# Decoder trunk of one attention/state-space layer and one S5 layer: where the first layer's activations and the low weight parts lie in memory, modulo 256 bytes

## The chip, the cores and the metric

The kernel runs on one NeuronCore of a Trainium2 chip. The metric is the device time of one execution in microseconds (us). Three runs of the kernel before took 1301.74, 1299.94 and 1299.41 us; the median is 1299.94 us.

## The reference

Two post-norm layers on an activation matrix of 256 positions by 2048 channels, in float32. Each one ends in `x <- LayerNorm(alpha * x + mixer(x))`.

```python
# layer 0
z, xbc, dt, q, k, v, gate = jnp.split(x @ w_in, SPLITS0, axis=-1)   # 2048 x 13344
y_a = ...   # state-space scan over conv(xbc), dt; gated by silu(z); RMS norm
y_b = moba_attention(rope(q), rope(k), v) * jax.nn.silu(gate)
h = jnp.concatenate([y_a, y_b], axis=-1) @ w_out                    # 4096 x 2048
# layer 1
u, gate = jnp.split(x @ w_in, 2, axis=-1)                           # 2048 x 4096
y = jax.nn.gelu(s5_ssm(u, ...))
ga, gb = jnp.split(y @ w_glu, 2, axis=-1)                           # 2048 x 4096
h = (ga * jax.nn.sigmoid(gb) * jax.nn.silu(gate)) @ w_out           # 2048 x 2048
```

The matrix products with `w_in`, `w_out` and `w_glu` are nearly all of the arithmetic, and the change concerns how TensorE reads the operands of those with the two `w_in`.

## The kernel before

**Split products.** TensorE multiplies float32r numbers. To keep float32 accuracy, each operand is split into a high part (the value copied as float32r) and a low part (the value minus its high part). A product is then three terms: high by high, high by low, low by high. ScalarE writes the high parts of the weights (L244), VectorE the low parts (L252). A unit is 512 KB of weights, loaded by one DMA into a tile `raw` and split into two tiles `wh` and `wl`, each 128 partitions by 1024 elements (4096 bytes in a partition). The pool `st` holds four buffers each of `raw`, `wh` and `wl`; units are taken in order, three ahead.

**Two ways to multiply.** A matmul has a stationary operand of 128 x 128, which a weight load (PEld in the profile) brings into the array, and a moving operand, which streams past it.

- In `pairmm` (L336 to L344) the weights stand and the activations move. The activations' high and low parts lie in one tile (`x2`, index 0 and 1, each 16 k-tiles of 256 positions). For each weight block there are two matmuls. The one at L340 has a block of `wh` standing and streams 512 columns: 256 of the high part, then 256 of the low part, 16,384 bytes further on. The one at L343 has the block of `wl` standing and streams the 256 columns of the high part. These two are called a pair here, the long step and the short step. All of the first layer's input projection but `v` is made so, 176 units with 8 pairs each, and the `u` half of the second layer's, but for its first 512 columns: 24 units with 8 pairs each. In the first 208 units (`TURNS`) the scheduler alternates long and short steps wherever both weight parts are there; the first 8 units (bank names `aux`) still run in groups of up to four of a kind. From unit 208 on all long steps of a unit come first, then all short ones.
- In `xmm` (L327 to L334) the activations stand and the weights move, 512 columns at a time. `v` in the first layer (4 products of 8 units, each unit 12 matmuls: 384 in all) and the products with `w_out`, `w_glu` and the `gate` half are made so.

**Where things lie.** The buffer `AB` is allocated at L479 as `xx` for the first layer's input, and later again for `ya`, `y5` and `gb1`. `CF` holds the other activations, `x1t` (the second layer's input) among them. In the allocation of the program before, every tile of `AB`, `CF`, `wh` and `wl` begins at 64 bytes modulo 256. Within them, k-tiles lie 1024 bytes apart and weight blocks 512 bytes, so that modulo 256 all slices of one tile begin alike. One thing differs: the function `low_tile` (L210 to L213) makes `wl` 256 bytes longer and, for the units listed in `weights_stand` (L208: those in which the weights stand), takes a view of it that begins `SHIFT` = 16 elements, 64 bytes, into the tile. So where weights stand, `wh` begins at the same place as x modulo 256, and `wl` 64 bytes behind x.

**What sets the order.** The instruction order is made by a scheduler from the program's dependencies. With one exception at the very start, TensorE's instruction stream is never held back by the others for long; the profile below shows it.

Of the kernel before, what the change touches and what calls it, by code (L numbers as in the profile page):

```python
# [10 lines left out]
F32R = mybir.dt.float32r  # L11
# [5 lines left out]
P = 128  # L17
S = 256
D = 2048
KT = D // P  # L20
UK = 2
# [3 lines left out]
FAST = [2, 3]  # L25
STEPS = [0, 1, 4, 2, 5, 6, 3, 7]
WARM0 = 10
SHIFT = 16
TURNS = 208
FIRST = 3  # L30
EPS = 1e-5
# [140 lines left out]
def trunk(tc, io, out):  # L172
# [4 lines left out]
    def nm(s):  # L177
        count[0] += 1
        return f"{s}_{count[0]}"

    with ExitStack() as top:
# [3 lines left out]
        st = enter(tc.tile_pool(name="st", bufs=4))  # L185
# [19 lines left out]
        def big(tag, shape, dt=F32):  # L205
            return slot.tile(shape, dt, tag=tag, name=nm(tag))

        weights_stand = set(range(80)) | {80 + 32 * h + i for h in range(4) for i in range(32) if i // 8 != 2} | set(range(280, 304))  # L208

        def low_tile(n=None):  # L210
            at = SHIFT if n in weights_stand else 0
            t = st.tile([P, UK * 512 + 4 * SHIFT], F32R, tag="wl", name=nm("wl"))
            return t[:, at : at + UK * 512].rearrange("p (k n) -> p k n", n=512)  # L213

        units = []
        for name in ("wi0", "wo0", "wi1", "wglu", "wo1"):
            units += [io[name][i] for i in range(io[name].shape[0])]
# [18 lines left out]
        def chained(engine, f, *args, **kw):  # L236
            with inline(engine):
                ins = f(*args, **kw)
            line[engine] = ins
            return ins  # L240
# [8 lines left out]
        def split(n, raw, wh, wl, high=None):  # L249
            high = high or split_high(n, raw, wh)  # L250
            with inline(V):
                low = V.tensor_tensor(wl, raw, wh.bitcast(F32), op=OP.subtract)  # L252
            if V in line:
                line[V] = low
            splits[n] = (high, low)
            ready[n] = (wh, wl)
            nsplit[0] += 1

        def split_to(i):
            while nsplit[0] <= min(i, len(units) - 1):  # L260
                n = nsplit[0]
                if n in early:
                    early.pop(n)()
                if n in special:
                    special.pop(n)(n)
                    continue
                raw = st.tile([P, UK, 512], F32, tag="raw", name=nm("raw"))
                if n == 0:
                    wh = st.tile([P, UK, 512], F32R, tag="wh", name=nm("wh"))
                    wl = low_tile(n)  # L270
                    for k in range(UK):
                        chained(nc.sync, nc.sync.dma_start, raw[:, k, :], units[n][:, k * 512 : k * 512 + 512])
                    for k in range(UK):
                        xpart(k)
                        chained(A, A.activation, wh[:, k, :], raw[:, k, :], AF.Copy)
                        chained(V, V.tensor_tensor, wl[:, k, :], raw[:, k, :], wh[:, k, :].bitcast(F32), op=OP.subtract)
                    ready[n] = (wh, wl)
                    nsplit[0] += 1
                    continue
                if n == FIRST + 1:  # L280
                    for e in (nc.sync, A, V):
                        line.pop(e, None)
                f = chained if nc.sync in line else lambda e, f, *a: f(*a)
                lastraw[0] = f(nc.sync, nc.sync.dma_start, raw.rearrange("p k n -> p (k n)"), units[n])
                at = room.get(n, n)
                if at in keep[1]:
                    wh, wl = (keep[0].tile([P, UK, 512], F32R, tag=f"{t}{at % 8}", name=nm(t)) for t in ("wh", "wl"))
                else:
                    wh, wl = st.tile([P, UK, 512], F32R, tag="wh", name=nm("wh")), low_tile(n)
                split(n, raw, wh, wl)  # L290

        jobs = deque()
# [55 lines left out]
        def product_pairs(hl, wide=None):  # L348
            ps = wide or banks()
            nu = CU if wide else CU // 2  # L350
            for u in range(nu):
                split_to(unit[0] + 3)
                wpair = ready.pop(unit[0])
                if not wide:
                    wpair = [quads(t) for t in wpair]
                nj, last = 2 if wide else 4, u == nu - 1
                steps = [(j, o) for j in range(nj) for o in range(len(ps))]
                if last:
                    steps = [(j, o) for o in range(len(ps)) for j in range(nj)]
                with inline(T):  # L360
                    for part in ([steps[:nj], steps[nj:]] if last else [steps]):
                        for terms, (j, o) in ([(t, s) for s in part for t in ((0,), (1,))] if unit[0] < TURNS else [(t, s) for t in ((0,), (1,)) for s in part]):
                            pairmm(ps, wpair, j, o, hl(u * nj + j), u == 0 and j == 0, last and j == nj - 1, terms)
                unit[0] += 1
                pump(nu - 1 - u)
            return ps
# [24 lines left out]
        def product(kind, hl, nu=CU, prelude=None, late=None):  # L391
            ps = banks()
            for u in range(nu):
                if prelude:
                    prelude(u)
                split_to(unit[0] + 3)
                wpair = ready.pop(unit[0])
                if kind == "w":
                    wmm(ps, u, nu, hl, wpair, late if u == 0 else None)
                else:  # L400
                    last = u == nu - 1
                    steps = [(j, o) for o in range(2) for j in range(UK)] if last else [(j, o) for j in range(UK) for o in range(2)]
                    for j, o in steps:
                        xmm(ps, o, wpair, j, hl(u * UK + j), u == 0 and j == 0, last and j == UK - 1)
                unit[0] += 1
                pump(nu - 1 - u)
            return ps
# [68 lines left out]
            for i in range(n):  # L476
                T.matmul(px[:m, 0 : z.shape[1]], z[:, 0:m], z, start=i == 0, stop=i == n - 1)

        xx = big("AB", [P, 2, KT, S], F32R)  # L479
        xh, xl = xx[:, 0], xx[:, 1]  # L480
        wb = [dram.tile([P, 1792], F32, name=f"wb{b}") for b in range(16)]
        qd = dram.tile([4, P, P], F32, name="qd")
# [8 lines left out]
        with ExitStack() as l0:  # L491
# [31 lines left out]
            def xpart(k):  # L523
                xr = xr0[k]
                chained(A, A.activation, xh[:, k, :], xr, AF.Copy)
                chained(V, V.tensor_tensor, xl[:, k, :], xr, xh[:, k, :].bitcast(F32), op=OP.subtract)
# [773 lines left out]
        with ExitStack() as l1:  # L1300
# [287 lines left out]
            forms, fx, gp, set0 = more["f"], more["x"], more["p"], more["s"]  # L1588

            def fast_unit(raws, second):  # L1590
                def go(n):
                    raw = st.tile([P, UK, 512], F32, tag="raw", name=nm("raw"))
                    lastraw[0] = nc.sync.dma_start(raw.rearrange("p k n -> p (k n)"), units[n])
                    if not second:
                        wh, wl = st.tile([P, UK, 512], F32R, tag="wh", name=nm("wh")), low_tile()
                        raws[0] = raw
                        split(n, raw, wh, wl)
                        return
                    wh, wl = (fx.tile([P, 1, 512], F32R, tag=t, bufs=2, name=nm(t)) for t in ("bh", "bl"))
                    ra = raws[0]  # L1600
                    ta, tb = (fx.tile([P, 2, 512], F32, tag="mix", bufs=2, name=nm("mix")) for _ in range(2))
                    V.tensor_tensor(ta, ra, raw[:, 1:2, :].to_broadcast([P, 2, 512]), op=OP.subtract)
                    V.tensor_tensor(tb[:, 0, :], ta[:, 1, :], ra[:, 0, :], op=OP.add)
                    V.tensor_tensor(tb[:, 1, :], raw[:, 0, :], tb[:, 0, :], op=OP.subtract)
                    got = [(wh, wl)]
                    A.activation(wh[:, 0, :], raw[:, 0, :], AF.Copy)
                    V.tensor_tensor(wl[:, 0, :], raw[:, 0, :], wh[:, 0, :].bitcast(F32), op=OP.subtract)
                    for t, pool, bufs in ((ta, fx, 2), (tb, st, 4)):
                        th = pool.tile([P, UK, 512], F32R, tag="wh", bufs=bufs, name=nm("wh"))
                        tl = low_tile() if pool is st else fx.tile([P, UK, 512], F32R, tag="wl", bufs=2, name=nm("wl"))  # L1610
                        high = A.activation(th, t, AF.Copy)
                        low = V.tensor_tensor(tl, t, th.bitcast(F32), op=OP.subtract)
                        got.append((th, tl))
                    splits[n] = (high, low)
                    ready[n] = got
                    nsplit[0] += 1
                return go
# [260 lines left out]
```

## Time and profile before

| | |
|---|---|
| median of three runs | 1299.94 us |
| profiled execution, its own time | 1299.05 us |
| span of the profiled execution (first to last instruction) | 1297.3 us |
| TensorE busy | 1289.6 us (99%) |
| weight loads busy (they overlap the matmuls) | 1093.0 us (84%) |
| VectorE, ScalarE, GpSimd busy | 1042.0, 705.5, 422.7 us |
| granted TensorE clock, mean | 1.000 |

Matmuls are pipelined: a matmul is shown as busy until its last result has been written, so the durations of neighbours overlap. What a matmul costs in a stream is the time from its start to the start of the next one, and that is called a step here. The chain of waits gives the same as the duration of its pieces, and the timeline gives starts to 0.01 us, so that steps are best read over several in a row.

### The profile page before, as it was taken

What the parts mean: (1) busy time and instruction counts of PE and PEld (TensorE: products, weight loads), DVE (VectorE), ACT (ScalarE), POOL (GpSimd) and SP (SyncE); (2) the same over time, 40 slices, a digit from 0 to 9 for tenths busy, and PEclk for the clock granted to TensorE, in tenths of its full rate; (3) what the DMA queues carried; (4) which work ended last, traced back from release to release, by engine and by line L of the source; (5) the groups of instructions that cost most, each with busy time, mean ns of one, the idle gap of its engine ahead of it and who ended that gap; (6) DMA issues with size and microseconds to landing.
All of it is one profiled execution on the core that took longest, in us unless ns stands there. A gap on an engine that the chain in (4) does not pass through costs nothing.

```text
span 1297.3 us, 21557 instructions
## 1 busy us (share of the span) xinstructions
PE 1289.6 (99%) x7998; PEld 1093.0 (84%) x7998; DVE 1042.0 (80%) x1575; ACT 705.5 (54%) x974; POOL 422.7 (33%) x665
## 2 busy tenths in 40 slices
PE   9999999999999999999999999999999999999998
PEld 8888888887888888888888888888888888888886
DVE  6879948797799888889878766749998868878876
ACT  6657669974644544544654345643356545554442
POOL 0150000133029659748788720034433200000100
PEclk9999999999999999999999999999999999999999
DMA  8545675455557757858967777398988665556862
GB/s 326 185 161 179 207 272 195 156 186 180 205 189 248 260 184 263 270 177 256 328 212 259 234 270 255 131 324 271 322 307 296 212 214 191 181 182 225 284 228 89
DMA packets 92106, 295.47 MB, mean 228 GB/s; under 512 B 11536, under 2 KB 18704, under 8 KB 91744
## 3 DMA queue, kind: packets, MB, share of 16 engines
q1 hardware_dynamic: 73696, 249.57, 55.9%
q0 software_dynamic: 8224, 32.81, 7.7%
q10 hardware_dynamic: 10080, 11.71, 3.0%
q8 instruction: 63, 1.03, 0.3%
q14 instruction: 43, 0.35, 0.1%
HBM read 272.78 MB, written 21.27 MB: 227 GB/s over the span
## 4 chain that ended last, share of the span: by engine, by line
PE 95%; POOL 2%; DVE 1%; DMA 1%; ACT 0%; issue 0%; SPq 0%; POOLq 0%; ACTq 0%
PE main L332 37%; PE main L340 25%; PE main L343 13%; PE more L1632 7%; PE main L1632 3%; PE main L1270 2%; PE aux L963 1%; PE aux L340 1%; POOL CF L579 1%; PE aux L864 1%; POOL CF L580 1%; PE enc L1390 1%; PE dec L1435 1%; PE aux L468 1%; PE aux L1050 1%; PE aux L1083 1%
## 5 line engine op out<-in xcount | busy, mean ns | idle before, releaser
L252 DVE TENSOR_TENSOR wl<-raw,wh 128x1024 fp32r<-128x1024 f32 x425 | 530.6, 1254 | 194.0 <-ACT wh L244 189.0
L244 ACT ACTIVATE wh<-raw 128x1024 fp32r<-128x1024 f32 x425 | 446.8, 1057 | 435.0 <-PE main L332 177.4
L340 PE MATMUL main<-AB,wh 128*128 128x512 f32 x1344 | 470.8, 394 | 0.0
L343 PE MATMUL main<-AB,wl 128*128 128x256 f32 x1344 | 376.3, 280 | 0.0
L340 PEld LDWEIGHTS main<-AB,wh 128*128 128x128 f32 x1344 | 252.3, 188 | 54.8 <-issue 1.2
L343 PEld LDWEIGHTS main<-AB,wl 128*128 128x128 f32 x1344 | 255.1, 190 | 0.7 <-issue 0.4
L332 PE MATMUL main<-wh,CF 128*128 128x512 f32 (+1 forms) x768 | 240.0, 391 | 0.0
L332 PE MATMUL main<-wh,AB 128*128 128x512 f32 x640 | 201.8, 392 | 0.0
L332 PEld LDWEIGHTS main<-wh,CF 128*128 128x128 f32 x768 | 143.7, 188 | 30.0
L332 PE MATMUL main<-wl,CF 128*128 128x512 f32 x384 | 149.5, 389 | 0.0
L332 PEld LDWEIGHTS main<-wh,AB 128*128 128x128 f32 x640 | 120.0, 188 | 25.8 <-issue 0.6
L793 POOL TENSOR_TENSOR c<-c 128x8 f32<-128x8 f32 (+2 forms) x192 | 121.8, 652 | 38.5 <-DMA wb<-c 31.0
L332 PE MATMUL main<-wl,AB 128*128 128x512 f32 x320 | 124.7, 390 | 0.0
L332 PEld LDWEIGHTS main<-wl,CF 128*128 128x128 f32 x384 | 72.1, 188 | 14.6
L1632 PE MATMUL more<-wh,AB 128*128 128x512 f32 x228 | 76.8, 391 | 0.0
L795 POOL TENSOR_TENSOR c<-c,c 128x4 f32<-128x4 f32 (+2 forms) x96 | 68.1, 709 | 7.4
L332 PEld LDWEIGHTS main<-wl,AB 128*128 128x128 f32 x320 | 60.1, 188 | 12.1
L1030 POOL TENSOR_TENSOR a<-a,b 64x512 f32<-64x512 f32 x16 | 28.7, 1796 | 112.9 <-DVE a L1029 93.8
L972 POOL TENSOR_TENSOR ssq<-ssq,c 128x256 f32<-128x256 f32 x16 | 22.0, 1373 | 111.0 <-ACT c L970 110.3
L796 POOL TENSOR_TENSOR c<-c,c 128x4 f32<-128x4 f32 (+2 forms) x96 | 53.8, 561 | 0.0
L340 PE MATMUL main<-CF,wh 128*128 128x512 f32 x192 | 50.4, 396 | 0.0
L1632 PEld LDWEIGHTS more<-wh,AB 128*128 128x128 f32 x228 | 42.7, 188 | 8.8
(355 smaller groups left out, 1634.8 us busy)
## 6 DMA issues: line engine op xcount, KB each, us to landing
raw<-in_wi SPq DMA_DIRECT2D x271, 512.0 KB, 4.1
raw<-in_wo SPq DMA_DIRECT2D x96, 512.0 KB, 4.4
raw<-in_wglu SPq DMA_DIRECT2D x64, 512.0 KB, 3.3
wt<-wb POOLq DMA_DIRECT2D x16, 896.0 KB, 7.2
a<-cumd SPq DMA_DIRECT2D x8, 512.0 KB, 6.0
bc<-in_s5bc SPq DMA_DIRECT2D x16, 256.0 KB, 4.5
bt<-in_s5bt SPq DMA_DIRECT2D x16, 256.0 KB, 5.4
lt<-qd SPq DMA_DIRECT2D x32, 128.0 KB, 5.2
```

The source lines that it names most:

```text
L244: ins = A.activation(wh, raw, AF.Copy)
L252: low = V.tensor_tensor(wl, raw, wh.bitcast(F32), op=OP.subtract)
L332: end = T.matmul((ps[o] if acc is None else acc)[:, cs], l[:, k, sl], r[:, j, cs], start=start and i == 0, stop=stop and i == 2, skip_grou ...
L340: T.matmul(ps[o].rearrange("p (a n) -> p a n", a=2), wh[:, j, sl], x2[:, :, k, :], start=start, stop=False, skip_group_check=True)
L343: T.matmul(ps[o][:, 0:S], wl[:, j, sl], x2[:, 0, k, :], start=False, stop=stop, skip_group_check=True)
L793: G.tensor_tensor(p[:, :, :, 0:m], cs[:, :, :, 1 : m + 1], cs[:, i, :, n : n + 1].unsqueeze(1).to_broadcast([P, 2, 4, m]), op=OP.mult)
L795: G.tensor_tensor(cs[:, 0, :, n + 1 : n + 1 + m], p0[:, 0, :, 0:m], p1[:, 1, :, 0:m], op=OP.subtract)
L796: G.tensor_tensor(cs[:, 1, :, n + 1 : n + 1 + m], p0[:, 1, :, 0:m], p1[:, 0, :, 0:m], op=OP.add)
L972: G.tensor_tensor(ssq, ssq, jk[:, f, :], op=OP.add)
L1030: turns.append(G.tensor_tensor(q[0:64], q[0:64], tm, op=OP.add))
L1270: end = T.matmul(ps[t], l[:, k, sl], r[:, j, :], start=k == 0 and i == 0, stop=k == KT - 1 and i == 2)
L1632: lastmm[0] = T.matmul(ps[name], l, r, start=start and i == 0, stop=last and i == 2, skip_group_check=True)
```

## The change

The long tile goes from the weights to the first layer's activations.

```diff
-SHIFT = 16
+SHIFT = 48
...
-        weights_stand = set(range(80)) | {80 + 32 * h + i for h in range(4) for i in range(32) if i // 8 != 2} | set(range(280, 304))
-
-        def low_tile(n=None):
-            at = SHIFT if n in weights_stand else 0
-            t = st.tile([P, UK * 512 + 4 * SHIFT], F32R, tag="wl", name=nm("wl"))
-            return t[:, at : at + UK * 512].rearrange("p (k n) -> p k n", n=512)
-
...
-                    wl = low_tile(n)
+                    wl = st.tile([P, UK, 512], F32R, tag="wl", name=nm("wl"))
...
-        xx = big("AB", [P, 2, KT, S], F32R)
+        xx = big("AB", [P, 2 * KT * S + 64], F32R)[:, SHIFT : SHIFT + 2 * KT * S].rearrange("p (a k s) -> p a k s", a=2, k=KT)
```

The other three uses of `low_tile` become plain `st.tile` calls in the same way. In the allocation of the new program `AB`, `CF`, `wh` and `wl` again begin at 64 bytes modulo 256, and the first layer's x 192 bytes further on, at 0. Places modulo 256 bytes, counted from where the moving operand begins:

| where | standing operand | before | now |
|---|---|---|---|
| first layer, pairs, long step's `wh` | weights | 0 | 64 |
| first layer, pairs, short step's `wl` | weights | 64 | 64 |
| first layer, `v` products | x, with `wh` or `wl` moving | 0 | 192 |
| second layer, pairs, `wh` | weights | 0 | 0 |
| second layer, pairs, short step's `wl` | weights | 64 | 0 |
| first layer, 32 small matmuls for `dt` | weights (`wdp`) | 0 | 64 |
| all other split products | | 0 | 0 |

On each of the five engines the instructions stand in the same order in both programs, with the same tiles, sizes and waits; only addresses differ. (Seven source lines are gone, so that what was L340 is L333 in the new program, and so on.)

More of the change, by code (lines that the diff above doesn't have):

```diff
@@ L288, in split_to @@
                 else:
-                    wh, wl = st.tile([P, UK, 512], F32R, tag="wh", name=nm("wh")), low_tile(n)
+                    wh, wl = st.tile([P, UK, 512], F32R, tag="wh", name=nm("wh")), st.tile([P, UK, 512], F32R, tag="wl", name=nm("wl"))
                 split(n, raw, wh, wl)
@@ L1594, in go @@
                     if not second:
-                        wh, wl = st.tile([P, UK, 512], F32R, tag="wh", name=nm("wh")), low_tile()
+                        wh, wl = st.tile([P, UK, 512], F32R, tag="wh", name=nm("wh")), st.tile([P, UK, 512], F32R, tag="wl", name=nm("wl"))
                         raws[0] = raw
@@ L1609, in go @@
                         th = pool.tile([P, UK, 512], F32R, tag="wh", bufs=bufs, name=nm("wh"))
-                        tl = low_tile() if pool is st else fx.tile([P, UK, 512], F32R, tag="wl", bufs=2, name=nm("wl"))
+                        tl = pool.tile([P, UK, 512], F32R, tag="wl", bufs=bufs, name=nm("wl"))
                         high = A.activation(th, t, AF.Copy)
```

## The prediction

> **What bounds the kernel now.** I read the page's first part first, then who waited for whom on TensorE, then the chain of waits.
>
> ```profile
> PE 1289.6 (99%) x7998; PEld 1093.0 (84%) x7998; DVE 1042.0 (80%) x1575; ACT 705.5 (54%) x974; POOL 422.7 (33%) x665
> PE aux L477 <- POOL D L472: 1.3, 1, 1.3
> PE aux L606 <- DVE CF L595: 0.7, 1, 0.7
> PE tail L1838 <- ACT raw L1819: 0.6, 1, 0.6
> PE 95%; POOL 2%; DVE 1%; DMA 1%; ACT 0%; issue 0%; SPq 0%; POOLq 0%; ACTq 0%
> PE main L332 37%; PE main L340 25%; PE main L343 13%; PE more L1632 7%; PE main L1632 3%; PE main L1270 2%; PE aux L963 1%; PE aux L340 1%; POOL CF L579 1%; PE aux L864 1%; POOL CF L580 1%; PE enc L1390 1%; PE dec L1435 1%; PE aux L468 1%; PE aux L1050 1%; PE aux L1083 1%
> ```
>
> TensorE waits for 2.6 us in all; the chain lies on it for 95% of the span. What one matmul step gains or loses is therefore gained or lost at the end, and nothing else on the core can hide it. The pairs (L340 with L343) make 38% of the chain. Their number comes from the groups of instructions by line, over the whole span:
>
> ```profile
> L340 PE MATMUL main<-AB,wh 128*128 128x512 f32 x1344 | 470.8, 394 | 0.0
> L343 PE MATMUL main<-AB,wl 128*128 128x256 f32 x1344 | 376.3, 280 | 0.0
> L340 PE MATMUL main<-CF,wh 128*128 128x512 f32 x192 | 50.4, 396 | 0.0
> L340 PE MATMUL aux<-AB,wh 128*128 128x512 f32 x64 | 20.6, 401 | 0.0
> ```
>
> So there are 1344 + 64 = 1408 pairs on the first layer's x and 192 on the second's. What a pair costs in steps, the chain shows; the columns are start in us, duration in us, and what, and a run of equal pieces has its count behind it.
>
> ```profile
> 490.00 0.23 PE main L340
> 490.23 0.12 PE main L343
> ...
> 491.97 0.12 PE main L343
> 492.08 10.93 PE main L332 x48
> ```
>
> The stretch from 490.00 to 492.08 holds six alternating pairs: 2.08 / 6 = 0.3467 us, 346.7 ns a pair, the long step 0.23 and the short step 0.12. The 48 matmuls behind it (`v`, x standing, 512 columns each) take 10.93 / 48 = 227.7 ns each. At that rate of columns a pair (768 columns) would take 1.5 x 227.7 = 341.6 ns. A pair thus carries about 5 ns more than its columns cost, about 7 us over 1408 pairs.
>
> Next, which load meets which stream, from the timeline (start, duration, engine):
>
> ```profile
> 299.92 0.39 PE L332 MATMUL main<-wl,AB 128*128 128x512 f32 x1
> 299.93 0.41 PEld L332 LDWEIGHTS main<-wh,AB 128*128 128x128 f32 x2
> ```
>
> The load for the next matmul begins 0.01 us after the matmul before it. So during a long step of an alternating pair TensorE loads the next `wl` block (64 bytes behind x now), and during a short step the next `wh` block (0 bytes behind x now). The change alters the second of these meetings, 0 to 64, and leaves the first.
>
> **The change part by part.** Instructions, order, sizes and waits stay the same, so no DMA, no queue and no other engine's work moves. The low tile's view costs nothing before or now: it is an address. Three terms are left, all of them steps on TensorE.
>
> *Term 1, the 1408 pairs.* The trace of before has places where other loads meet short steps. In the first units long and short steps run in groups (timeline of TensorE alone):
>
> ```profile
> 14.96 1.10 PE L340 MATMUL aux<-AB,wh 128*128 128x512 f32 x4
> 15.89 0.62 PE L343 MATMUL aux<-AB,wl 128*128 128x256 f32 x4
> 16.34 0.40 PE L340 MATMUL aux<-AB,wh 128*128 128x512 f32 x1
> ```
>
> Four short steps take 16.34 - 15.89 = 0.45 us, 112.5 ns each; under three of them a `wl` block is loaded, 64 behind x. Against the 117 ns or so in an alternating pair (346.7 less 230 for the long step, the rate of the row quoted next) that is 4 ns less. But the four long steps ahead of them, three of which meet a `wh` load at 0, take (15.89 - 14.96) / 4 = 232.5 ns. The second layer's pairs come in groups of eight (chain):
>
> ```profile
> 860.23 1.84 PE main L340 x8
> 862.07 0.94 PE main L343 x8
> 863.01 1.16 PE main L340 x5
> ```
>
> Here the short steps, seven of eight with a load at 64, take 0.94 / 8 = 117.5 ns, the long ones, seven of eight with a load at 0, 1.84 / 8 = 230 ns. Last, 256-column steps with every load at 0, at the very end of the program (chain; below it the weight loads of such steps, count and duration min/median/max):
>
> ```profile
> 1286.37 1.45 PE part L332 x12
> L332 PEld LDWEIGHTS part<-wh,CF x8: 192/192/192, 1286.1 to 1287.4; 128*128 128x128 f32 x8
> ```
>
> These take 1.45 / 12 = 120.8 ns. So a 256-column step with a load at 0 costs 117 to 121 ns, with a load at 64 from 112.5 to 117.5. The ends of this term are then: no gain (117 and 117.5 are the same), and a pair at the rate of its columns, 341.6, or lower still with 227.7 + 112.5 = 340.2 ns, a gain of 6.5 ns a pair, 1408 x 6.5 = 9.2 us. Below the first end a loss cannot be excluded (a rival, below). The nearest row is the group of four: same x, same pool of weights, same layer, load at 64. Its short step gains 117 - 112.5 = 4.5 ns. Since the second layer's row shows that the gain need not come, I take two thirds of it, 3 ns, a choice and not a reading: 1408 x 3 = 4.2 us gained.
>
> The Trainium skill, page "TensorE: Matmul & The Clock Gate", section "Back-to-back issue gap", puts a warm isolated matmul at N / 2.4 + 2.5 ns, so 215.8 and 109.2. By that a pair could fall to 325 ns, and the gain would reach 1408 x 21.7 = 31 us; but no row quoted here has a 512-column step under 227 ns, so that rule is not what a placement can bring back.
>
> *Term 2, the 384 `v` matmuls.* x stands at 192 behind the moving weights, not at 0. Their number: over the first 635 us the groups by line have
>
> ```profile
> L332 PE MATMUL main<-wh,AB 128*128 128x512 f32 x256 | 80.9, 392 | 0.0
> L332 PE MATMUL main<-wl,AB 128*128 128x512 f32 x128 | 49.9, 390 | 0.0
> ```
>
> 256 + 128 = 384. Nothing in the trace shows a load at 192. The ends: their 227.7 ns stay, since 512 columns last far longer than a load; or they go to the slowest 512-column run above, 232.5 ns, 384 x 4.8 = 1.8 us lost. A gain is not excluded either, but the 227.7 ns are the fastest 512-column rate of the rows here, so I give it nothing. I take 0.3 us lost, near the first end, as the load has room.
>
> *Term 3, the 192 pairs of the second layer.* Their `wl` goes from 64 to 0. The short steps go from 117.5 at best nowhere, at worst to the 120.8 of the row with every load at 0: 192 x 3.3 = 0.6 us lost. I take 0.3 us. Their last `wl` load under a long step is one in eight pairs and is within that. The 32 small matmuls for `dt` are too few to matter.
>
> Sum: -4.2 + 0.3 + 0.3 = -3.6 us. From the profiled execution's 1299.05 us that makes 1295.4 us. The median of the runs, 1299.94, is 0.9 us above the profiled one, and the forecast is made against it: 1299.94 - 3.6 = 1296.3 us.
>
> **The rivals.**
>
> *Same: the pair keeps its price.* Add up the three arrangements above. Alternating: 346.7 ns a pair. Groups of four: (16.34 - 14.96) / 4 = 345 ns. Groups of eight: (863.01 - 860.23) / 8 = 347.5 ns. The short step is 112.5 in one and 117.5 in another, yet the pair costs nearly the same, as if what is saved in a short step were paid in a long one. If the extra 5 ns belong to the pair (say, to the jump from the high to the low part within the long step) and not to the address, nothing happens: within 1.5 us of 1299.9. For it speaks that the loads meeting a long step at 64 are not shorter but longer than those at 0 (groups by line, weight loads, mean ns in the middle):
>
> ```profile
> L343 PEld LDWEIGHTS main<-AB,wl 128*128 128x128 f32 x1344 | 255.1, 190 | 0.7 <-issue 0.4
> L340 PEld LDWEIGHTS main<-AB,wh 128*128 128x128 f32 x1344 | 252.3, 188 | 54.8 <-issue 1.2 <-ACT b L942 0.2
> ```
>
> 190 against 188 ns: 64 is no place free of stalls. Against it speaks that in all three arrangements one load in two lies at 0, so that they cannot tell "the pair costs 5 ns" from "each load at 0 costs 5 ns, wherever it falls". In the new program no load of a first-layer pair lies at 0, and this is what it will decide. The Trainium skill, page "SBUF — State Buffer", section "Who interferes with whom", says that TensorE has two independent read ports for the moving operand and the weight load and never waits on anyone; by that rule this rival is the truth and the change does nothing. The rows agree in part only: 256-column steps differ, 112.5 to 120.8 ns, with nothing else waited for. I give it 0.32.
>
> *Slower: the stall moves into the long step and grows.* The group of four shows that a short step of 112.5 ns is followed by nothing faster: the first long step behind it runs from 16.34, and the four before ran at 232.5. If both loads at 64 give short steps of 117.5, as in the second layer, and long steps of 232.5, the pair costs 350 ns, 3.3 more than now: 1408 x 3.3 = 4.6 us lost, and with the worst of terms 2 and 3 (1.8 + 0.6) 7 us, 1306.9 at most. A milder form is that the pairs gain nothing and terms 2 and 3 come at their worst: 1299.94 + 2.4 = 1302.3 us. It decides as soon as the pairs gain less than 2.4 / 1408 = 1.7 ns. For it: at 0 every 512-column stream of `v` runs at the fastest rate of the program, so moving x away from it can only harm those. Against: the long step's own meeting, with `wl` at 64, is unchanged by the edit. I give it 0.18.
>
> *More than forecast:* each load at 0 costs a pair all of its extra, and the pair falls to 340.2 ns: -9.2 + 0.6 = -8.6 us, 1291.3 us. It is the far end of the forecast and has 0.15 of its chance.
>
> **How the numbers follow.** A measurement of this kernel can tell about 0.2% from no change, 2.6 us. Forecast and its far end: 0.50, all of it below 1297.3 us. Same: 0.32. Slower: 0.18, split between 1302.3 and up to 1306.9. The range runs from the far end, 1291.3, less half a microsecond for the terms taken as losses, 1290.8, up to 1302.6, which takes in the milder slow form; left out are what is beyond the far end and the moved stall, together less than 0.2. As cases of both signs do not hold most of the chance, the likeliest one's own range is only noted: 1291 to 1297.3.
>
> **What would show it.** In the profile after, six alternating pairs on x in the chain should take 2.06 us (343.7 ns a pair), not 2.08, with the gain in the short step; over a stretch of 48 pairs 16.5 us, not 16.64. The `v` runs of 48 should stay at 10.9 to 11.0 us; 11.16 would be term 2 at its worst. The second layer's groups of eight short steps should stay at 0.94 to 0.97 us. The order of all else should be the same and TensorE's waits within 1 us of the 2.6. Wrong is the forecast if the pair stays at 346 to 347 ns (the same-rival), or if the short step falls and the long one rises by as much or more (the slower one).

## The result, and the profile after

The changed kernel takes 1308.16 us in the median (four runs, 1307.70 to 1308.24); the kernel before took 1300.04 us beside it (four runs, 1299.41 to 1301.74). The ratio is 1.0066, with a 95% interval from 1.0052 to 1.0080. The change makes the kernel slower by about 8 us, where a gain of 3.6 us was forecast; the result lies above the range. The profiled execution of the new kernel has an own time of 1308.24 us and a span of 1306.4 us, 9.1 us more than the span before.

The page of the kernel after, with the lines that answer to those of before, and who waited for whom on TensorE:

```profile
PE 1298.6 (99%) x7998; PEld 1093.1 (84%) x7998; DVE 1042.3 (80%) x1575; ACT 706.9 (54%) x974; POOL 423.1 (32%) x665
PE main L325 37%; PE main L333 28%; PE main L336 14%; PE more L1625 7%; PE main L1625 3%; PE main L1263 2%; PE aux L956 1%; PE aux L333 1%; PE aux L857 1%; PE enc L1383 1%; PE dec L1428 1%; PE aux L461 1%; PE aux L1043 1%; PE aux L1076 1%; PE aux L336 1%; PE dec L1424 0%
PE aux L470 <- POOL D L465: 1.3, 1, 1.3
PE aux L333 <- ACT wh L237: 0.8, 1, 0.8
PE tail L1831 <- ACT raw L1812: 0.6, 1, 0.6
```

TensorE is busy 9.0 us longer (1298.6 against 1289.6) and waits for 2.7 us as it did for 2.6: a wait of 0.8 us for a high part near the start is new, and one of 0.7 us for VectorE is gone. The other engines' busy times are the same to within 1.4 us. So the time came on TensorE itself, with the same 7998 matmuls and no more to wait for. The shares of the chain by line are no measure here: L333 and L336 have 42% where L340 and L343 had 38%, but part of that is that the chain of before left TensorE for a while (POOL 2%, DVE 1%, DMA 1%) and this one did not.

The groups by line mislead as well, in the other direction:

```profile
L333 PE MATMUL main<-AB,wh 128*128 128x512 f32 x1344 | 479.2, 399 | 0.0
L336 PE MATMUL main<-AB,wl 128*128 128x256 f32 x1344 | 378.2, 281 | 0.0
L333 PEld LDWEIGHTS main<-AB,wh 128*128 128x128 f32 x1344 | 252.7, 188 | 62.5 <-issue 1.2
L336 PEld LDWEIGHTS main<-AB,wl 128*128 128x128 f32 x1344 | 252.4, 188 | 0.8 <-issue 0.4
```

The `wl` loads became shorter in the mean, 188 ns where they took 190, and still the program became slower. The duration of a load says nothing here about what it costs the stream beside it. The steps do. (A piece of the chain of waits runs from the end of one matmul to the end of the next, where the timeline and the table of steps below go by starts. Over a run of alike pairs both give the same price; at the edge of a group of steps they differ.) In the chain of the kernel after (start, duration, what), the same place as before:

```profile
490.20 0.23 PE main L333
490.44 0.12 PE main L336
...
492.20 0.12 PE main L336
492.32 0.23 PE main L333
...
499.04 10.99 PE main L325 x48
```

Six pairs last from 490.20 to 492.32, 2.12 us or 353.3 ns a pair; before it was 2.08 us, 346.7 ns. The forecast had 2.06 us, 343.7 ns. The 48 `v` products behind take 10.99 us, 229.0 ns each; before 227.7.

Added up over the whole program from the starts in the two traces, to the nanosecond:

| steps | count | before, us | after, us | difference |
|---|---|---|---|---|
| long steps on x, `main` | 1344 | 311.88 | 318.68 | +6.80 |
| short steps on x, `main` | 1344 | 158.78 | 160.47 | +1.69 |
| x standing, `wh` moving (`v` among them) | 724 | 166.84 | 167.44 | +0.60 |
| x standing, `wl` moving (`v` among them) | 362 | 82.35 | 82.44 | +0.09 |
| second layer, long steps | 192 | 45.29 | 45.31 | +0.02 |
| second layer, short steps | 192 | 23.32 | 23.56 | +0.24 |

The sum is 9.4 us; the spans differ by 9.1, as the rest of the program comes out 0.3 us shorter. Nine tenths of it are the pairs, and four fifths of what the pairs lost lie in the long step: 232.1 ns to 237.1 ns in the mean. (The means contain the few pairs at which other matmuls come between.)

### The profile page after: what moved, and what is told of

Same layout as the page of the kernel before. It is cut to its first block, busy times and chain, and to the rows that moved or that the text cites. A ratio compares the mean times of both kernels' runs of the same rounds, so it can differ in the third digit from the quotient of the medians.

```text
span 1306.4 us, 21557 instructions
## 1 busy us (share of the span) xinstructions
PE 1298.6 (99%) x7998; PEld 1093.1 (84%) x7998; DVE 1042.3 (80%) x1575; ACT 706.9 (54%) x974; POOL 423.1 (32%) x665
## 4 chain that ended last, share of the span: by engine, by line
PE 98%; DVE 0%; DMA 0%; SPq 0%; ACT 0%; issue 0%
PE main L325 37%; PE main L333 28%; PE main L336 14%; PE more L1625 7%; PE main L1625 3%; PE main L1263 2%; PE aux L956 1%; PE aux L333 1%; PE aux L857 1%; PE enc L1383 1%; PE dec L1428 1%; PE aux L461 1%; PE aux L1043 1%; PE aux L1076 1%; PE aux L336 1%; PE dec L1424 0%
## 5 line engine op out<-in xcount | busy, mean ns | idle before, releaser
L333 PE MATMUL main<-AB,wh 128*128 128x512 f32 x1344 | 479.2, 399 | 0.0
L336 PE MATMUL main<-AB,wl 128*128 128x256 f32 x1344 | 378.2, 281 | 0.0
L333 PEld LDWEIGHTS main<-AB,wh 128*128 128x128 f32 x1344 | 252.7, 188 | 62.5 <-issue 1.2
L336 PEld LDWEIGHTS main<-AB,wl 128*128 128x128 f32 x1344 | 252.4, 188 | 0.8 <-issue 0.4
L786 POOL TENSOR_TENSOR c<-c 128x8 f32<-128x8 f32 (+2 forms) x192 | 130.2, 696 | 34.2 <-DMA wb<-c 26.6
L788 POOL TENSOR_TENSOR c<-c,c 128x4 f32<-128x4 f32 (+2 forms) x96 | 60.6, 631 | 7.4
L789 POOL TENSOR_TENSOR c<-c,c 128x4 f32<-128x4 f32 (+2 forms) x96 | 58.1, 605 | 0.0
L333 PE MATMUL main<-CF,wh 128*128 128x512 f32 x192 | 50.4, 397 | 0.0
```

What stands on the lines that cost most here:

```text
L333: T.matmul(ps[o].rearrange("p (a n) -> p a n", a=2), wh[:, j, sl], x2[:, :, k, :], start=start, stop=False, skip_group_check=True)
L336: T.matmul(ps[o][:, 0:S], wl[:, j, sl], x2[:, 0, k, :], start=False, stop=stop, skip_group_check=True)
L786: G.tensor_tensor(p[:, :, :, 0:m], cs[:, :, :, 1 : m + 1], cs[:, i, :, n : n + 1].unsqueeze(1).to_broadcast([P, 2, 4, m]), op=OP.mult)
L788: G.tensor_tensor(cs[:, 0, :, n + 1 : n + 1 + m], p0[:, 0, :, 0:m], p1[:, 1, :, 0:m], op=OP.subtract)
L789: G.tensor_tensor(cs[:, 1, :, n + 1 : n + 1 + m], p0[:, 1, :, 0:m], p1[:, 0, :, 0:m], op=OP.add)
```

## The experiments

All twelve kernels keep the program's instructions and move operands by multiples of 64 bytes; the last one also changes the order in the second layer. A kernel's places are written as (`wh`, `wl`), in bytes behind the moving x, modulo 256: before is (0, 64), after (64, 64).

Theories were wanted that say what sets the price of a pair. Those that the expectations speak of are these. *Meeting*: each load that meets a stream has a fixed price by its own place behind x. *Distance*: what counts is how far `wl` lies behind `wh`, 64 before and 0 after; x has no part in it. *Own*: what counts is where the standing block lies against the operand that streams past it in its own matmul. *Alike*: a pair costs 353.3 ns whenever both parts lie at one place. *Absolute*: the addresses count, not their relation to x. *Rhythm* (called *relation* in the last four), which took shape after the first four runs: both places behind x together allow a few steady patterns, each with its own price, and what comes between picks one of them.

The prices below are steps taken from the starts in each trace. "Held" are the prices at which long stretches ran, and the mean is over the 176 units of the first layer (by how interrupted pairs are counted it shifts by up to 0.3 ns). The column behind it is what the pairs should cost by that mean, (mean less 347.1) x 1408.

| run | (`wh`, `wl`) | held, ns a pair | mean, ns | 1408 pairs, us | median, us | kernel before beside it, us | ratio, 95% interval |
|---|---|---|---|---|---|---|---|
| before | 0, 64 | 346.7 | 347.1 | 0 | 1300.04 | | |
| after | 64, 64 | 353.3 | 352.9 | +8.2 | 1308.16 | 1300.04 | 1.0066 [1.0052, 1.0080] |
| p0_0 | 0, 0 | 346.7, 353.3 | 349.6 | +3.5 | 1302.51, one run | 1298.53, one run | |
| p0_128 | 0, 128 | 346.7, 350 | 348.2 | +1.5 | 1299.96, one run | 1298.53, one run | |
| p64_0 | 64, 0 | 340, 350, 353.3 | 345.7 | -2.0 | 1304.35, one run | 1298.53, one run | |
| p64_128 | 64, 128 | 350, 353.3 | 350.3 | +4.5 | 1315.27, one run | 1298.53, one run | |
| h64 | 64, 0 | 340, 350, 353.3 | 348.0 | +1.3 | 1300.41 | 1298.37 | 1.0012 [1.0002, 1.0022] |
| h128 | 128, 0 | 352.0 | 351.9 | +6.8 | 1305.64 | 1298.37 | 1.0052 [1.0037, 1.0067] |
| h192 | 192, 0 | 340, in 15 units 350 | 341.2 | -8.3 | 1292.53 | 1298.37 | 0.9952 [0.9937, 0.9967] |
| p0_192 | 0, 192 | 346.7, 350, 351.1 | 349.6 | +3.5 | 1302.72 | 1298.37 | 1.0030 [1.0019, 1.0041] |
| x64_all0 | 192, 192 | 348.9, 353.3 | 352.0 | +6.9 | 1307.55 | 1298.57 | 1.0069 [1.0054, 1.0084] |
| x128_all0 | 128, 128 | 351.1 | 351.1 | +5.6 | 1305.95 | 1298.57 | 1.0054 [1.0041, 1.0068] |
| p192_0_by_x | 192, 0 | 340, in 13 units 350 | 341.2 | -8.3 | 1303.35 | 1298.57 | 1.0041 [1.0028, 1.0055] |
| h192_turns | 192, 0 | 340, in 15 units 350 | 341.2 | -8.3 | 1292.38 | 1298.57 | 0.9948 [0.9936, 0.9961] |

Where x stands and weights move, a kernel that moves x or all of `wl` has other places too. By the starts, one of the `v` steps takes 227.4 ns in the kernel before, 229.2 in the kernel after, 233.2 in x64_all0 and 232.4 in x128_all0, in the last three of which x lies 192, 64 and 128 behind the moving weights. In p64_0, p64_128 and p192_0_by_x (233.3, 231.8 and 234.1 ns) the moved `wl` slows later products as well, so that of these three only the price of the pair is compared, not the time. In the runs p0 and h the second layer's 192 pairs have the first layer's new places; the column of costs leaves them out.

### First four: other places for wl

p0_0 and p0_128 are the kernel before with `wl` at another place (the tile keeps a padding of 256 bytes); `SHIFT` is 0 in p0_0, as shown, and 32 in p0_128:

```diff
-SHIFT = 16
+SHIFT = 0
-            t = st.tile([P, UK * 512 + 4 * SHIFT], F32R, tag="wl", name=nm("wl"))
+            t = st.tile([P, UK * 512 + 64], F32R, tag="wl", name=nm("wl"))
```

p64_0 and p64_128 are the kernel after with unused tiles of 192 and 64 bytes (p64_128: 64 and 192) ahead of and behind the `wl` buffers:

```diff
                     wh = st.tile([P, UK, 512], F32R, tag="wh", name=nm("wh"))
+                    st.tile([P, 48], F32, tag="gap0", bufs=1, name="gap0")
                     wl = st.tile([P, UK, 512], F32R, tag="wl", name=nm("wl"))
+                    st.tile([P, 16], F32, tag="gap1", bufs=1, name="gap1")
```

**p0_0**

> The kernel before with SHIFT = 0: in the first layer's pairs wh lies 0 and wl 0 bytes behind x (modulo 256), and the second layer's wl at 0. Three theories for the new price of an alternating pair, 353.3 ns instead of 346.7. MEETING (the price goes by where the block being loaded lies against the x that streams at that moment; a long step meets wl, a short step wh): the short step meets 0 as in the kernel before, the long step meets 0 instead of 64; groups of long steps with that meeting ran at 230 to 235 ns, so 347 to 352 ns a pair. DISTANCE (the price goes by how far wl lies from wh, the two blocks that are loaded by turns; x does not matter): the distance is 0 as in the new kernel, so 353.3 ns a pair and about 1309.5 us. OWN (the price goes by where the block that stands in the long step, wh, lies against x: 0 good, 64 bad): 346.7 ns a pair, about 1300 us.

Measured: neither one price nor the other, but both, in turn. Two stretches of the chain of p0_0; the first runs at 353.3 ns (three pairs in 1.06 us), the second at 346.7 (six pairs in 2.08 us):

```profile
65.31 0.24 PE main L340
...
66.37 0.24 PE main L340
...
138.07 0.23 PE main L340
...
140.15 0.23 PE main L340
```

The first stretch has a long step of 0.24 us in every third pair, the second repeats after two pairs. One placement has two prices, so the price cannot be a sum of two meetings with a price each (*meeting* falls), nor does a distance of 0 fix it at 353.3 (*distance* and *alike* fall).

**p64_128**

> The new kernel with every wl buffer of the pool moved 64 bytes on by a spacer: in the first layer's pairs wh lies 64 and wl 128 bytes behind x. The products in which x stands have their wl elsewhere too, so only the price of a pair is compared. MEETING: the short step meets 64 as in the new kernel, the long step 128, a place not tried: 118 + 230 or more, 348 to 353 ns a pair. DISTANCE: 64, as in the kernel before, 346.7 ns. OWN: wh at 64, 353.3 ns.

Measured: mostly 350 ns (six pairs in 2.10 us), mean 350.3. The distance between `wh` and `wl` is 64 as in the kernel before, and the price is not 346.7: the second count against *distance*. The run of 48 `v` products shows why its time is not compared, 11.31 / 48 = 235.6 ns each:

```profile
99.84 0.23 PE main L335
...
101.94 0.23 PE main L335
...
298.88 11.31 PE main L327 x48
```

**p64_0**

> The same with a spacer of 192 bytes: wh 64 and wl 0 bytes behind x, distance -64. MEETING: the short step meets 64, the long step meets 0, both the bad way by the rows so far: 353 ns a pair or more. DISTANCE: not 0, so under 353.3; if only its size counts 346.7 ns. OWN: 353.3 ns.

Measured: three prices in one program. In the chain of p64_0:

```profile
31.96 0.23 PE main L335
...
34.08 0.23 PE main L335
...
105.45 0.23 PE main L335
...
107.56 0.23 PE main L335
...
112.81 0.87 PE aux L463 x8
...
114.03 0.23 PE main L335
...
116.07 0.23 PE main L335
```

The first six pairs take 2.12 us (353.3 ns). The second six take 2.11 us (the rows have a grain of 0.01 us; the starts in the trace give 350). Then eight small matmuls come between, and the six pairs behind them take 2.04 us, 340 ns, in the same arrangement of addresses and with nothing waited for. So 340 can be had with `wh` away from x, which *own* excludes, and what chooses between the prices lies in what comes between.

**p0_128**

> The kernel before with SHIFT = 32 and the pad kept: wh 0 and wl 128 bytes behind x, distance 128; the second layer's wl at 128. MEETING: the short step meets 0 as in the kernel before, the long step 128: 344 to 350 ns a pair, open. DISTANCE: 128 is as far as can be, so 346.7 ns or less. OWN: wh at 0, 346.7 ns.

Measured: 346.7 and 350, mean 348.2, and 1299.96 us in the one run. *Distance* and *own* had 346.7 at most, and the 350 goes against both. With `wh` at x's place the pair never came under 346.7, wherever `wl` lay (0, 64, 128, later 192).

### Next four: wh moves in place of wl

h64, h128 and h192 are the kernel before with the shift given to `wh` and none to `wl`, so that x, `v` and all other products lie as before. They use `SHIFT` 16, 32 and 48:

```diff
-SHIFT = 16
+SHIFT = 48
         def low_tile(n=None):
+            t = st.tile([P, UK * 512], F32R, tag="wl", name=nm("wl"))
+            return t.rearrange("p (k n) -> p k n", n=512)
+
+        def high_tile(n=None):
             at = SHIFT if n in weights_stand else 0
-            t = st.tile([P, UK * 512 + 4 * SHIFT], F32R, tag="wl", name=nm("wl"))
+            t = st.tile([P, UK * 512 + 64], F32R, tag="wh", name=nm("wh"))
...
-                    wh, wl = st.tile([P, UK, 512], F32R, tag="wh", name=nm("wh")), low_tile(n)
+                    wh, wl = high_tile(n), low_tile(n)
```

p0_192 is p0_0 with `SHIFT = 48`.

**h64**

> The kernel before with the shift taken from wl and given to wh: x 0, wh 64, wl 0 bytes behind x where weights stand (both layers); x stands for v as in the kernel before. The same relations as p64_0, but x at another address and v untouched. RHYTHM (each pair of places allows its own few locked rhythms of the alternating steps, and each interruption of the row of pairs picks one of them; only the relations modulo 256 count): the same rhythms as in p64_0, 340, 350 and 353 ns a pair, in shares that may differ, mean 343 to 350 ns, v at 227 ns, so 1294 to 1304 us. MEETING with a fixed price per meeting (long step at 0, short step at 64): one price throughout, no change of it at interruptions. ABSOLUTE (x at 0 modulo 256 itself is what was costly in the new kernel, not the relation): x is at 64 as before, so about 347 ns throughout and 1300 us.

Measured: the same three prices as p64_0 (340, 350, 353.3), in other shares, mean 348.0, and 1300.41 us. p64_0 came to the relation (64, 0) by moving `wl` with x at 0, h64 by moving `wh` with x at 64. That the set is the same speaks for the relation and against *absolute*. Which of the three a given stretch gets is not the same in the two programs (12 long stretches of 23 at 340 in p64_0, 6 in h64), so that the relation does not fix the pick.

**h128**

> The same with wh 128 and wl 0 bytes behind x. RHYTHM: a set of rhythms of its own, in steps of 3.3 ns from 340 to 357 ns; if its rhythms are few the price is the same all along. MEETING: one price throughout. DISTANCE (128 between wh and wl, as in p0_128, x of no account): p0_128's prices, 347 and 350 ns, about 1300 us.

Measured: one price, 352.0 ns, mean 351.9, and 1305.64 us. *Distance* had 347 and 350. The pattern is five pairs long, 1.76 us in the chain of h128, or 352.0 ns a pair; a count of pairs that is no multiple of five comes out anywhere from 350 to 353:

```profile
99.80 0.23 PE main L344
...
101.56 0.23 PE main L344
```

**h192**

> The same with wh 192 and wl 0 bytes behind x. RHYTHM: a set of its own between 340 and 357 ns. DISTANCE: wl lies 64 behind wh, as in the kernel before, so 346.7 ns throughout, 1300 us. MEETING: one price throughout.

Measured: 340 ns in nearly all units, six pairs in 2.04 us:

```profile
99.86 0.23 PE main L344
...
101.90 0.23 PE main L344
```

The kernel takes 1292.53 us (1290.44 to 1295.03), ratio 0.9952 with an interval from 0.9937 to 0.9967 to the kernel before. It beats both kernels. The long step is about 226 ns and the short one 114: a pair costs a little less than the 341.6 ns of its 768 columns at the rate of the `v` run, and the extra of a pair, of which the prediction spoke, is gone. So the extra can be avoided by a placement; the changed kernel took the wrong one. (*Distance* had 346.7 for h192.)

**p0_192**

> The kernel before with SHIFT = 48 and the pad kept: wh 0 and wl 192 bytes behind x. RHYTHM: a set of its own between 340 and 357 ns. DISTANCE: -64 as in p64_0, so that one's prices, 340, 350 and 353 ns. OWN (wh at 0 is what counts): 346.7 ns throughout.

Measured: 346.7 to 351.1, mean 349.6, and 1302.72 us, where *own* had 346.7 throughout. h192 and p0_192 have the same pair of places with the two parts exchanged. So a displacement of 192 in itself neither helps nor harms; it depends on which of the two parts has it.

### Last four: the same relation by other addresses

x64_all0 and x128_all0 are the kernel after with `SHIFT` 16 and 32 in place of 48, so that x lies elsewhere and both weight parts at one place behind it. p192_0_by_x is the kernel after with `SHIFT = 16` and the unused tiles of p64_128, which gives h192's relation with x, `wl` at other addresses. h192_turns is h192 with alternating steps in the second layer, too:

```diff
-TURNS = 208
+TURNS = 10000
```

**x64_all0**

> The new kernel with SHIFT = 16 instead of 48: x lies 64 bytes on, so that wh and wl both lie 192 bytes behind it (64 ahead), the mirror of the change; v has x standing at 64. So far the price of a pair follows the place of wh, which the short step meets: 192 gave 340 ns (h192), 0 gave 347 to 352, 64 gave 340 to 353, 128 gave 352. RELATION (the two places modulo 256 against x decide, by a set of rhythms of their own): the short step meets 192 as in h192, the long step 192 as in p0_192 (347 to 352): between 340 and 350 ns a pair, 1290 to 1304 us. ALIKE (what was wrong with the new kernel is that both weights lie alike against x, distance 0, whatever the place): 353.3 ns throughout, 1307 us.

Measured: 353.3 and 348.9, mean 352.0, and 1307.55 us. That misses the band of *relation*, 340 to 350, which had been put together from what each of the two places cost in other placements. *Alike* came near, but not with 353.3 throughout. Where it runs at 353.3 it is not the steady pattern of the kernel after, which repeats in each pair, but one that repeats after three pairs, 1.06 us:

```profile
96.87 0.23 PE main L333
...
97.93 0.23 PE main L333
...
98.99 0.23 PE main L333
```

**x128_all0**

> The new kernel with SHIFT = 32: wh and wl both 128 bytes behind x; v has x standing at 128. RELATION: the short step meets 128 as in h128 (352 ns), the long step 128 as in p64_128 and p0_128 (347 to 353): 350 to 354 ns. ALIKE: 353.3 ns throughout.

Measured: one price, 351.1 in a pattern of three pairs, and 1305.95 us; *alike* had 353.3. With p0_0, x64_all0 and the kernel after, that makes four placements with both parts alike, (0, 0), (64, 64), (128, 128) and (192, 192), at means of 349.6, 352.9, 351.1 and 352.0: having both parts alike costs something in each, but not one price.

**p192_0_by_x**

> The places of h192 (wh 192, wl 0 bytes behind x) made in another way: x 64 bytes on in its longer tile, every wl buffer 64 bytes on by a spacer. Where x stands, its place against the moving weights changes, so the total is not comparable; the price of a pair is. RELATION: 340 ns in most units, as in h192, and 350 in the rest. ABSOLUTE (the addresses themselves count): another price.

Measured: 340 ns in 132 of 176 units and 350 in 13, mean 341.2, the same as h192 to the tenth. Six pairs in 2.04 us again:

```profile
94.93 0.23 PE main L335
...
96.97 0.23 PE main L335
...
295.98 6.80 PE main L327 x29
```

x and both weight parts lie 64 bytes further on here than in h192: *absolute* falls, and only the places behind x count for the price. The last row shows what it costs elsewhere: 29 `v` products at 234.5 ns each. The whole kernel takes 1303.35 us and is slower than the kernel before, although its pairs cost as little as h192's.

**h192_turns**

> h192 with TURNS raised beyond the last unit, so that the second layer's pairs alternate too, as the first layer's do. RELATION: those 192 pairs fall from about 347 to 340 ns a pair too, 1.2 us less than h192, about 1291.3 us. If the order is of no account: as h192, 1292.5 us. A low part that is not ready when its turn comes would stall TensorE: later than h192.

Measured: the second layer's pairs now cost 340 ns too, five pairs in 1.70 us:

```profile
881.99 0.23 PE main L344
...
883.69 0.23 PE main L344
```

Summed over the trace, the steps of the second layer's 192 pairs come to 67.2 us (44.40 + 22.79), where h192 in its groups had 69.6 (46.18 + 23.42) and the kernel before 68.6. Yet 1292.38 us (1290.39 to 1293.96) cannot be told from h192's 1292.53: the 2.4 us between the two sums are less than the spread of the runs of either, 3.6 and 4.6 us, and the 1.2 us that were expected are not shown in the time.

### What holds

Of the theories only *rhythm* is left. It was put at risk by h64, p192_0_by_x and h192_turns alone, which had to show the prices of p64_0 or h192 again and did; elsewhere its expectation was a band of prices, and x64_all0 missed its band. Each of thirteen traces (all in the table but h192_turns) has 23 stretches of more than 20 pairs with nothing between. In twelve of them six pairs near the start of a stretch cost the same as the last six, to 1.7 ns, in all 23; in h128 the same holds for whole patterns of five pairs. From one stretch to the next the price changed up to 15 times of 22 (p64_0 15, h64 and p0_128 14, p0_0 9), and never in before and after. So a placement allows a set of steady patterns; an interruption picks one; it lasts to the next interruption. The patterns repeat after one, two, three or five pairs, and most prices lie on a grid of 3.3 ns (340, 346.7, 350, 353.3); those off it (348.9, 351.1, 352.0) belong to patterns of three or five pairs. (0, 64) allows one price alone, 346.7, (64, 64) 353.3, (128, 0) 352.0 and (128, 128) 351.1. (192, 0) nearly always falls into 340.

Two more things can be read from these traces. That 256 bytes is a period can be read from the kernel before: its four `wl` buffers lie 4352 bytes apart, so that from one unit to the next `wl` moves on by 256 bytes modulo 512, and the price stays 346.7 over stretches of up to 84 pairs. And the other engines' work in the same memory does not set the price by coming and going: VectorE and ScalarE are busy for 80% and 54% of that kernel's time, with starts and stops all along such stretches.

What is not settled is why: no view shows how a load and a stream delay each other within TensorE, so which placement allows which patterns could be measured but not derived, and what in an interruption makes the pick was not tried. Eleven of the sixteen placements in steps of 64 were tried; (64, 192), (128, 64), (128, 192), (192, 64), (192, 128) and finer steps were not.

## Why the prediction was wrong

**What bounds the kernel** was right. TensorE waits for 2.7 us, nothing hides a longer step, and the 9.1 us of the span are the sum of the steps but for 0.3. That the pairs carry an extra which placement can take away was right too: h192 took it away, 341.2 ns a pair in the mean, close to the 340.2 of the far end.

**Term 1 failed, in its sign.** The step was this: the short step's load goes from 0 to 64, the group of four has short steps of 112.5 ns with loads at 64, so the pair gains two thirds of the 4.5 ns. It measured +6.3 ns a pair in place of -3: 6.80 + 1.69 us are 8.5 us over the 1344 `main` pairs (the 64 of the first units, with a wait among them, left out). Two things were wrong with it. The first is that half a pair was priced. The reading of the short steps was close: by the starts in the trace the four take 453 ns, 113.3 each, though the rows, with a grain of 0.01 us, give four steps only to 2.5 ns. But the four long steps beside them took 933 ns, 233.3 each, where an alternating pair in that trace has about 229.6. The pair of the group thus cost 346.5 ns and the alternating one 346.7: there was no gain to carry over, which the prediction's own rival "same" had added up from the rows as 345 against 346.7. The same group in the timeline of the kernel after:

```profile
15.39 1.10 PE L333 MATMUL aux<-AB,wh 128*128 128x512 f32 x4
16.33 0.62 PE L336 MATMUL aux<-AB,wl 128*128 128x256 f32 x4
16.79 0.39 PE L333 MATMUL aux<-AB,wh 128*128 128x512 f32 x1
```

Its short steps take 114.5 ns and its long ones 234.3 by the starts, 348.8 ns a pair, where the alternating pairs of that program take 353.3. So a group of four does not tell what an alternating pair costs, before or after.

The second, and the graver, is behind the first: the idea that a meeting has a price that can be carried from one arrangement to another. The long step's own load (`wl` at 64) is the same before and after, and yet the long step took 5 ns more. p0_0 and p64_0 show it directly: the same meetings, at two and three prices. A price belongs to a pattern of a pair or more, and only a row with that pattern has it. No row of before had both parts at 64, so the honest end of this term on the side of a loss was as far as the end on the side of a gain, and the range left that out: it held 1.8 + 0.6 us of losses in terms 2 and 3 and gave term 1 a gain or nothing outside a rival.

**Term 2** (the `v` products with x at 192): 0.3 us taken, 1.8 at worst; 0.7 us measured, 0.60 + 0.09 by the table of steps. Right in sign and between its ends, though nearer the middle than "the load has room" had it.

**Term 3** (the second layer's pairs): 0.3 us taken, 0.6 at worst; 0.26 measured. The groups of eight of the kernel after, short steps 0.95 / 8 = 118.8 ns in place of 117.5, long ones 1.84 / 8 = 230 ns as before:

```profile
859.39 0.95 PE main L336 x8
860.34 1.84 PE main L333 x8
862.18 0.71 PE main L336 x6
```

**The rival "same"** was wrong in its reason, that the extra belongs to the pair and not to the address. The eleven placements have means between 341.2 and 352.9 ns a pair. It leaned on the Trainium skill, page "SBUF — State Buffer", section "Who interferes with whom", by which TensorE's two read ports are independent and TensorE never waits on anyone. What the prediction drew from that, that the change does nothing, does not hold here: with the same instructions in the same order, addresses alone made the kernel between 0.48% faster (h192, 0.9937 to 0.9967) and 0.69% slower (x64_all0, 1.0054 to 1.0084). Whether it is the read of the memory or something within TensorE that gives way, no run tells. From the formula of the Trainium skill, page "TensorE: Matmul & The Clock Gate", section "Back-to-back issue gap", for an isolated matmul the prediction had worked out an estimate of 325 ns a pair; the best pattern found has 340, with about 226 ns for 512 columns, so it was right to leave that out of its ends.

**The rival "slower"** had the right place: the stall moved into the long step. It was 353.3 ns a pair in place of the 350 that it added up, with a long step of 237.1 ns in the mean where it had 232.5, and so 1308 us where it gave 1306.9 at most. What spoke against it ("the long step's own meeting, with `wl` at 64, is unchanged by the edit") was the argument that failed, and it was that argument which kept its chance at 0.18.

## What to carry to other kernels

When loads and streams of TensorE overlap all the time, where the standing operand lies behind the moving one modulo 256 bytes was worth up to 4% of such a pair of steps here (340 to 353.3 ns), and it is cheap to try: move the one operand that is used in no other product (here `wh` and `wl` of the units whose weights stand), one multiple of 64 at a time, and read the price over long stretches of the chain. Don't infer the price of one placement from parts of another; run all of them. And look at the products that share the operand: moving x was the wrong lever even where the pairs gained, since it displaced everything that streams past x (`v` went from 227.4 to between 229.2 and 233.2 ns a step).

## What else the runs showed of the hardware

**A price that lasts.** The two or three prices of one placement, each kept for as long as nothing came between, were not expected. Over a whole kernel they show as a mean that no single stretch has, such as 345.7 ns in p64_0.

**A short loss of clock at the fastest kernel.** h192's runs spread over 4.6 us (1290.44 to 1295.03), those of the kernel before beside it over 1.9 (1297.90 to 1299.84). Its profiled execution, the slowest of the four, has this in the table by stretches (the last three columns are the granted clock, the DMA share and GB/s); below it is the same stretch of the kernel before:

```profile
86.00:90.00 4.00, 3.79 (x14) 3.25 (x15) 3.96 (x8) 1.77 (x4) 0.72 (x1) 0.57 0.42 139
```

```profile
86.00:90.00 4.00, 3.71 (x22) 3.30 (x23) 3.96 (x7) 1.77 (x4) 0.72 (x1) 1.00 0.38 139
```

The granted clock is 0.57 against 1.00, 14 matmuls against 22. In the chain of h192 a long step there takes 0.43 us and a short one 0.21, until the clock is back:

```profile
87.56 0.43 PE main L344
87.99 0.21 PE main L347
...
90.39 0.23 PE main L344
90.62 0.12 PE main L347
```

These pairs come right behind a few small matmuls that had waited for VectorE. The five pairs from 87.56 to 90.39 take 2.83 us where 1.70 would do at 340 ns. The profile of h192_turns has the granted clock at 0.57 as well, from 88 to 92 us. It is part of why h192 stays behind the 8.3 us that its pairs are worth: 5.8 us are measured in the medians, and 7.9 us from its fastest run to the median of before. What differs there is how long TensorE stood idle. The kernel before waited once, 0.73 us, as its pairs ran on until just before the small matmuls; h192 came to the end of its pairs 1 us earlier and waited twice, 0.81 and 0.85 us. From 84 to 86 us its TensorE is busy for 0.55 us, that of the kernel before for 1.56:

```profile
84.00:86.00 2.00, 0.55 (x3) 0.13 (x1) 1.28 (x3) 0.00 (x0) 0.61 (x1) 1.00 0.01 2
```

```profile
84.00:86.00 2.00, 1.56 (x9) 1.08 (x8) 1.21 (x3) 0.00 (x0) 0.69 (x1) 1.00 0.04 14
```

h192_turns waited twice in the same place (0.86 and 0.85 us), and of the fourteen traces these two alone have the clock down in the midst of the program. That the idle time is the cause is likely by this and was not tried.
